# An encoder trunk on one core: ScalarE takes half of each look from turn 23 on, the two halves of the weight sums run one after the other, and outputs and mixes are reordered

## The chip, the cores and the metric

The kernel runs on one core of one Trainium2 chip. The metric is the device time of one execution in microseconds (us), taken as the median of several runs. A profiled execution gives a trace of every instruction of the five engines: PE (TensorE; PEld is its loading of weights), DVE (VectorE), ACT (ScalarE), POOL (GpSimd) and SP (SyncE, which issues the DMAs).

## The reference

For each of two sequences (prompt, 1024 tokens; sample, 2048 tokens) one layer is computed:

```python
h = rms_norm(x, norm_pre)
z = einsum('btd,de->bte', h, w_in)
u_pool, g_pool, q, k, v, g_attn, q_x, g_x = split(z)
pool_out = multiscale_pool(u_pool, pool_w, pool_scale) * silu(g_pool)
q, k = rope(rms_norm(q)), rope(rms_norm(k))        # 8 query heads, 2 key heads, 64 wide
attn_out = softmax(q k^T / 8) v * silu(g_attn)      # every query sees every key
x_out = softmax(q_x k_m^T / 8) v_m * silu(g_x)      # 256 memory tokens, 4 heads
y = einsum('bte,ed->btd', concat(pool_out, attn_out, x_out), w_out)
return x + rms_norm(y, norm_post)
```

## The kernel before

The first part (to 709 us) makes normed and transposed tokens, projects them with w_in and writes queries, keys, values and gates to scratch in HBM; the scheduler of the language orders it. The second part (attention, output projection) has its order written out by hand, one queue for each engine, and the change lies there.

A *pair* is 256 queries: the sample has 8 pairs, which go first, the prompt 4. A pair has three *groups*: kind 0 and kind 1 are the two halves of the self-attention heads, kind 2 is the memory attention; they run in the order 0, 2, 1 (2, 0, 1 in the first pair). A *turn* is two chunks of 128 keys of one group, so a sample pair has 8 + 1 + 8 = 17 turns and a prompt pair 4 + 1 + 4 = 9. Turn n issues, in this order on every engine:

- *look*: the softmax needs the largest score of each query before its weights are made. PE writes the scores of 128 queries with 512 keys for two heads into the tile N (1024 columns, two PSUM banks, one buffer), and DVE reduces them to the largest ones in `nb` (L191; `top` for kind 2). Two looks are made in a turn, for a group that comes later; the second is issued after the weights.
- `sums(kb+1)`: the odd chunk of the turn before is added to the running sum z of the weights. In the sample POOL adds the first 512 columns and DVE the other 512 (CUT = (0, 512), L235 and L236); in the prompt DVE adds all 1024.
- `weights(k)`, `weights(k+1)`: PE makes scores in the tile S, ACT makes P = exp(S) (L223; five buffers of P).
- the second look, then `sums(k)`.
- on one turn in two from turn 23 on a piece of the output projection into `py` (`project`, 4 pieces of 3 matmuls in the sample, 8 in the prompt; after its last piece ACT squares the bank, L386), on the other `values`: PE adds P times V of four chunks into `acc` (L248). Before turn 23 values of two chunks are made in every turn.
- one turn after a group's last, `totals`: PE multiplies the finished z by ones (L257). Columns 0 to 511 come first, and those are POOL's.

Work that hangs on a turn is put in by `at(turn + fraction, ...)`: fraction 0 before the first look, .1 after it, .4 before the projection, .6 at the turn's end. `take` multiplies `acc` by the gate (L263), `turned`, `inverse` and `spread` turn the totals into factors (L267, L272 and L275, then two DMAs by way of HBM, `rows` and `gz`), `mix_out` multiplies them in (L292, POOL) and `high` and `low` split the product for the projection (L295 ACT, L299 POOL). `scale`, `norm` and `out` finish an output tile (L398 DVE, L402 DVE and L405 POOL, L414 ACT and L415 POOL).

Of the kernel before, what the change touches and what calls it, by code (L numbers as in the profile page):

```python
# [23 lines left out]
def encoder(ctx, tc, I, O):  # L24
# [25 lines left out]
    DVM = [scratch(f"dvm{s}", [128, 2, 4, 64]) for s in range(2)]  # L50

    const = ctx.enter_context(tc.tile_pool(name="const", bufs=1))
    ident = const.tile([128, 128], F32, name="ident")
    make_identity(nc, ident)
    mhalf = const.tile([128, 8], F32, name="mhalf")
    nc.vector.memset(mhalf, -0.5)

    def rsqrt(pool, ss, n, count, tag):

# [71 lines left out]
    class Group:  # L131
# [36 lines left out]

        def largest(self, n):
            a, lane = self.pieces[n]
            S = psn.tile([128, 1024], F32, name="N", tag="N")
            if self.kind == 2:
                for x in range(2):
                    for j in range(2):
                        h = slice(64 * j, 64 * j + 64)
                        nc.tensor.matmul(S[:, 512 * j + 256 * x:512 * j + 256 * x + 256],
                                         lhsT=self.q[h, 0, 256 * lane + 128 * x:256 * lane + 128 * x + 128],
                                         rhs=K2[0][h, lane, 0], start=True, stop=True)  # L180
                S = S.rearrange("p (j x k) -> p j x k", j=2, x=2)
                out = self.top[:, 0:8].rearrange("p (j i x) -> p j i x", j=2, i=2)[:, :, lane]
            else:
                for j in range(2):
                    h = slice(64 * j, 64 * j + 64)
                    nc.tensor.matmul(S[:, 512 * j:512 * j + 512],  # L186
                                     lhsT=self.q[h, 0, 128 * lane:128 * lane + 128],
                                     rhs=KH[self.kind][h, 512 * a:512 * a + 512], start=True, stop=True)
                S = S.rearrange("p (j k) -> p j k", j=2)
                out = self.nb[:, a].rearrange("p (j i) -> p j i", j=2)[:, :, lane]  # L190
            nc.vector.tensor_reduce(out=out, in_=S, axis=AX.X, op=ALU.max, negate=True)  # L191
            if n == len(self.pieces) - 1:
                self.shift()

# [30 lines left out]
        def sums(self, k):  # L225
            if k == 0:
                return
            if k == 1:
                self.z = dbl.tile([128, 2, 512], F32, name="z", tag="z")
            flat = "p j q -> p (j q)"  # L230
            z, P = self.z.rearrange(flat), self.P[k].rearrange(flat)
            a = self.P[0].rearrange(flat) if k == 1 else z
            cut = CUT[self.s]
            if cut:
                nc.gpsimd.tensor_tensor(out=z[:, :cut], in0=a[:, :cut], in1=P[:, :cut], op=ALU.add)  # L235
            nc.vector.tensor_tensor(out=z[:, cut:], in0=a[:, cut:], in1=P[:, cut:], op=ALU.add)  # L236

        def values(self, ks):

# [48 lines left out]
    def store_mix(slot, pair, c, a, b, v="p (c t q) -> p c t q"):  # L288
# [11 lines left out]

        after = (0, 0, pair.s, pair.s)[c // 2]
        begin = max(slot, pair.free + after)
        at(begin + 1.4, high)
        at(begin + 1.6, low)

    class Pair:

# [39 lines left out]
    class Output:  # L347
# [34 lines left out]
            nc.tensor.matmul(ps, lhsT=ml, rhs=wo_hi[:, c, cols], start=False, stop=final)  # L382

        def square(self, h):
            junk = own.tile([128, 512], mybir.dt.bfloat16, name="junk2", tag="junk2")
            nc.scalar.activation(out=junk, in_=self.ps[h], func=AF.Square, scale=D ** -0.5,  # L386
                                 accum_out=self.ss[:, h:h + 1])

# [10 lines left out]

        def norm(self):  # L400
            s1 = dbl.tile([128, 1], F32, name="s1", tag="s1")
            nc.vector.scalar_tensor_tensor(out=s1, in0=self.ss[:, 0:1], scalar=EPS, in1=self.ss[:, 1:2],  # L402
                                           op0=ALU.add, op1=ALU.add)
            self.r = dbl.tile([128, 1], F32, name="rs", tag="rsy")
            nc.gpsimd.tensor_tensor(out=self.r, in0=s1, in1=mhalf[:, 0:1], op=ALU.pow)  # L405

# [54 lines left out]
    for pair in pairs:  # L461
# [5 lines left out]
        for g in pair.groups:  # L467
            wait = first[g] + g.chunks // 2 + (2 if pair.last else 3)
            if pair is pairs[0] and g.kind != 1:
                wait += 3  # L470
            at(wait + 0.6, g.mix_out, wait + 1, pair)
        at(max(ends) + (3 if pair.last else 7), open_fill, pair)
    value_runs, sums_at = {}, {}
    for g in groups:
# [4 lines left out]
        while k < c:  # L479
            run = 1 if 2 < n + k < first[pairs[1].groups[0]] + 6 else 2  # L480
            value_runs[n + k + run - 1] = g, list(range(2 * k, min(2 * k + 2 * run, 2 * c)))
            k += run
        at(n + max(c, run) + 0.1, g.take)
        sums_at[n + c] = g
        at(n + c + 1.1, g.turned)
        if g in pairs[-1].groups:
            at(n + c + (1.4 if g.kind < 2 else 2.1), g.inverse)
            at(n + c + (1.4 if g.kind < 2 else 2.1), g.spread)
        else:
            at(n + c + (1.4 if g.kind < 2 else 2.6), g.inverse)  # L490
            at(n + c + (2.1 if g.kind < 2 else 3.1), g.spread)
    for c in range(NC):
        at(int(2.5 * c + 1), load_w_out, c)
        for h in range(2):
# [32 lines left out]
    def look(turn):  # L527
        if looks.get(turn):
            g, n = looks[turn].pop(0)
            g.largest(n)  # L530

    order = {mybir.EngineType.PE, mybir.EngineType.Activation, mybir.EngineType.DVE,
             mybir.EngineType.Pool, mybir.EngineType.SP}
# [7 lines left out]

    with ExitStack() as p1:
        one = p1.enter_context(tc.tile_pool(name="p1one", bufs=1))
        two = p1.enter_context(tc.tile_pool(name="p1two", bufs=2))
        big = p1.enter_context(tc.tile_pool(name="p1big", bufs=2))

# [411 lines left out]
    def project(turn):  # L958
# [3 lines left out]
        for _ in range(PIECES[turns[turn][0].s] if turn < len(turns) else 8):  # L962
            out, h, c, start, final = fill.pop(0)
            out.piece(h, c, start, final, turn >= looked)
            if final:
# [4 lines left out]
                else:  # L970
                    at(turn + 1.1, out.scale, h)
                if h == 1:
                    at(turn + (0.6 if end else 1.6), out.norm)
                    for x in range(2):
                        if out.last:
                            at(turn + 0.6, out.out, x, None)
                        else:
                            at(turn + 2.4 + x, out.out, x, None if end else turn + 3.2 + x)
                break

    with tc.manual_schedule(engines=order):
# [69 lines left out]
```

## Time and profile before

| what | us |
|---|---|
| median of three runs | 1746.3 (1745.69 to 1746.43) |
| the profiled execution, device time | 1745.43 |
| its span from first to last instruction | 1743.6 |
| PE busy | 1697.3 (97%) |
| DVE busy | 1116.8 (64%) |
| POOL busy | 844.3 (48%) |
| ACT busy | 656.7 (38%) |

Busy PE does not mean PE at its peak: matmuls overlap, and one that starts late is drawn longer. So what PE loses is read from the distance between the starts of its matmuls, beside the list of waits. In the lists, "PEld N L186 <- DVE nb L191: 37.5, 88, 0.8" says that the weight loads of line 186 sat behind idle time 88 times, 37.5 us in all and 0.8 us at most, that a DVE instruction of line 191 ended.

### The profile page before, as it was taken

Reading aid. Unit: us, or ns where it says so; the run is one execution under the profiler, and the core shown is the slowest. Engines: PE = TensorE matmul, PEld = TensorE weight load, DVE = VectorE, ACT = ScalarE, POOL = GpSimd, SP = SyncE. Lnnn points to the kernel's source line nnn. Section 1 sums busy time; section 2 is a strip of 40 time slices with the busy share of each in tenths; the row PEclk is TensorE's granted clock in tenths of the full one; section 3 lists DMA queues with packets and bytes.
Section 4 is the critical chain, followed back from the end, with each engine's and each line's share of the span. In section 5 each row is a group of like instructions: output and inputs, shape, how many; then the busy total and the mean of one; then the engine's idle time right before and its main releaser. Section 6 shows DMA issues by size and latency. Waiting matters only on the chain. (4 is left out here: it accounts for less than half of the span.)

```text
span 1743.6 us, 25303 instructions
## 1 busy us (share of the span) xinstructions
PE 1697.3 (97%) x9400; PEld 1168.0 (67%) x9400; DVE 1116.8 (64%) x1434; ACT 656.7 (38%) x978; POOL 844.3 (48%) x778
## 2 busy tenths in 40 slices
PE   7899999999999999999999999999999999999998
PEld 6889889798898986544555555555555555566566
DVE  6754316552164424799878787877777757876862
ACT  5533225332252211445444344444343433443441
POOL 4555205570054610499666575767666663331331
PEclk9999999999999999999999999999999999999999
DMA  7643634436443393612121212112111143323222
GB/s 256 177 132 87 186 94 135 128 89 172 113 124 91 110 217 85 181 62 86 49 73 61 68 53 76 56 49 77 48 58 55 61 127 110 103 80 109 68 91 91
DMA packets 151851, 178.27 MB, mean 102 GB/s; under 512 B 20896, under 2 KB 120368, under 8 KB 151728
## 3 DMA queue, kind: packets, MB, share of 16 engines
q1 hardware_dynamic: 151728, 176.65, 34.0%
q8 instruction: 74, 1.21, 0.3%
q14 instruction: 49, 0.40, 0.1%
HBM read 121.26 MB, written 55.20 MB: 101 GB/s over the span
## 5 line engine op out<-in xcount | busy, mean ns | idle before, releaser
L191 DVE TENSOR_REDUCE nb<-N 128x2 f32<-128x1024 f32 x320 | 390.3, 1220 | 215.7 <-PE N L186 215.0
L223 ACT ACTIVATE P<-S 128x1024 f32<-128x1024 f32 x344 | 334.6, 1023 | 436.5 <-PE S L221 174.0
L235 POOL TENSOR_TENSOR z<-z,P 128x512 f32<-128x512 f32 x224 | 324.2, 1447 | 160.2 <-ACT P L223 140.4
L248 PE MATMUL acc<-P,V 128*64 128x512 f32 (+1 forms) x1472 | 320.3, 575 | 1.5
L236 DVE TENSOR_TENSOR z<-z,P 128x512 f32<-128x512 f32 (+1 forms) x272 | 269.3, 990 | 4.5 <-ACT P L223 4.3
L614 PE MATMUL pz<-hT_hi,w_hi 128*128 128x512 f32 x592 | 235.2, 397 | 1.7 <-ACT vmst L884 0.8
L615 PE MATMUL pz<-hT_lo,w_hi 128*128 128x512 f32 x592 | 232.8, 393 | 0.0
L616 PE MATMUL pz<-hT_hi,w_lo 128*128 128x512 f32 x592 | 231.5, 391 | 0.1
L248 PEld LDWEIGHTS acc<-P,V 128*64 128x64 f32 x1472 | 95.3, 137 | 170.7 <-issue 130.7
L221 PE MATMUL S<-q,DH 64*128 64x512 f32 x1280 | 201.6, 392 | 0.0
L63 POOL TENSOR_TENSOR rs<-rs,mhalf 128x4 f32<-128x4 f32 (+2 forms) x76 | 83.6, 1103 | 210.4 <-DVE rs L61 207.3
L186 PE MATMUL N<-KH,q 64*128 64x512 f32 x640 | 157.0, 487 | 12.4 <-DVE nb L191 11.0
L186 PEld LDWEIGHTS N<-KH,q 64*128 64x128 f32 x640 | 59.8, 183 | 153.2 <-DVE nb L191 86.4
L614 PE MATMUL pz<-w_hi,hT_hi 128*128 128x384 f32 (+1 forms) x416 | 141.6, 341 | 3.8 <-ACT hT_hi L68 3.8
L615 PE MATMUL pz<-w_lo,hT_hi 128*128 128x384 f32 (+1 forms) x416 | 140.7, 338 | 0.9 <-DVE w_lo L69 0.8
L616 PE MATMUL pz<-w_hi,hT_lo 128*128 128x384 f32 (+1 forms) x416 | 140.6, 339 | 0.0
L380 PE MATMUL py<-wo_hi,mix 128*128 128x512 f32 x336 | 139.0, 414 | 0.0
L69 DVE TENSOR_TENSOR w_lo<-wraw,w_hi 128x3072 fp32r<-128x3072 f32 (+2 forms) x21 | 67.8, 3227 | 107.3 <-ACT w_hi L68 106.9
L221 PEld LDWEIGHTS S<-q,DH 64*128 64x128 f32 x1280 | 120.1, 185 | 23.6 <-issue 2.4
L382 PE MATMUL py<-wo_hi,mix 128*128 128x512 f32 x336 | 131.6, 392 | 0.1
L381 PE MATMUL py<-wo_lo,mix 128*128 128x512 f32 x336 | 131.5, 391 | 0.0
L614 PEld LDWEIGHTS pz<-hT_hi,w_hi 128*128 128x128 f32 x592 | 111.1, 188 | 29.1 <-issue 4.5
(152 smaller groups left out, 2436.3 us busy)
## 6 DMA issues: line engine op xcount, KB each, us to landing
wraw<-w_in SPq DMA_DIRECT2D x15, 1536.0 KB
dg<-gst SPq DMA_DIRECT2D x48, 256.0 KB
q<-dq SPq DMA_DIRECT2D x24, 512.0 KB
gz<-rows SPq DMA_DIRECT2D x72, 128.0 KB
x<-x_sample SPq DMA_DIRECT2D x16, 512.0 KB
xr<-x_sample SPq DMA_DIRECT2D x16, 512.0 KB
y_sample<-xr SPq DMA_DIRECT2D x32, 256.0 KB
dq<-qst SPq DMA_DIRECT2D x96, 64.0 KB
```

The costliest lines, as they stand in the source:

```text
L186: nc.tensor.matmul(S[:, 512 * j:512 * j + 512], lhsT=self.q[h, 0, 128 * lane:128 * lane + 128], rhs=KH[self.kind][h, 512 * a:512 * a + 512 ...
L191: nc.vector.tensor_reduce(out=out, in_=S, axis=AX.X, op=ALU.max, negate=True)
L221: nc.tensor.matmul(S[:, at + x:at + x + w], lhsT=K, rhs=self.q[h, qx, x:x + w], start=False, stop=n == 2, skip_group_check=True)
L223: nc.scalar.activation(out=self.P[k].rearrange("p j q -> p (j q)"), in_=S, func=AF.Exp)
L235: nc.gpsimd.tensor_tensor(out=z[:, :cut], in0=a[:, :cut], in1=P[:, :cut], op=ALU.add)
L236: nc.vector.tensor_tensor(out=z[:, cut:], in0=a[:, cut:], in1=P[:, cut:], op=ALU.add)
L248: nc.tensor.matmul(self.acc[64 * j:64 * j + 64, x], lhsT=v, rhs=P[:, j, x], start=(k, i) == (0, 0), stop=k == self.chunks - 1, skip_group_ ...
L380: nc.tensor.matmul(ps, lhsT=mh, rhs=wo_hi[:, c, cols], start=first, stop=False)
L382: nc.tensor.matmul(ps, lhsT=ml, rhs=wo_hi[:, c, cols], start=False, stop=final)
L614: nc.tensor.matmul(ps, lhsT=sh, rhs=mh, start=c == 0, stop=False)
L615: nc.tensor.matmul(ps, lhsT=sh, rhs=ml, start=False, stop=False)
L616: nc.tensor.matmul(ps, lhsT=sl, rhs=mh, start=False, stop=c == n - 1)
```

## The change

Seven things are changed.

- From turn 23 on, a look of kind 0 or 1 is shared: ACT copies the second bank of N to a tile `look` in SBUF, DVE reduces the first bank from PSUM (half A) and then the copy (half B). `square` writes its unused output to the same tile.
- In `sums` DVE's half is issued first, and POOL's half waits for it (`behind`), in every chunk but a group's last.
- `norm` adds its two sums on POOL in place of DVE.
- In the prompt, `norm`, `out` and `store` come up to one turn sooner, and `high` and `low` of four of the eight columns about one turn sooner.
- `turned` of kinds 0 and 1 comes before the first look in place of after it; `take` of kind 2 at the end of its turn.
- `inverse` and `spread` of kind 2 come about one turn later, but for the last pair, and its `mix_out` one turn later.
- The identity for the transposes is kept in the first part's pool only.

```diff
+    def behind(later, first):
+        tc.add_manual_dep(later.ins, first.ins.name,
+                          mybir.DependencyInfo(mybir.DependencyClass.Sync, mybir.DependencyReason.DATA),
+                          reason="one after the other")
...
-        def largest(self, n):
+        def largest(self, n, shared=False):
...
-            nc.vector.tensor_reduce(out=out, in_=S, axis=AX.X, op=ALU.max, negate=True)
+            if shared and self.kind < 2:
+                t = own.tile([128, 1, 512], F32, name="look", tag="look")
+                c = nc.scalar.copy(out=t[:, 0], in_=S[:, 1])
+                m = nc.vector.tensor_reduce(out=out[:, 0:1], in_=S[:, 0:1], axis=AX.X, op=ALU.max, negate=True)
+                tc.declare_no_dep(m.ins, c.ins, reason="two reads, in two banks")
+                nc.vector.tensor_reduce(out=out[:, 1:2], in_=t, axis=AX.X, op=ALU.max, negate=True)
+            else:
+                nc.vector.tensor_reduce(out=out, in_=S, axis=AX.X, op=ALU.max, negate=True)
...
+            v = nc.vector.tensor_tensor(out=z[:, cut:], in0=a[:, cut:], in1=P[:, cut:], op=ALU.add)
             if cut:
-                nc.gpsimd.tensor_tensor(out=z[:, :cut], in0=a[:, :cut], in1=P[:, :cut], op=ALU.add)
-            nc.vector.tensor_tensor(out=z[:, cut:], in0=a[:, cut:], in1=P[:, cut:], op=ALU.add)
+                e = nc.gpsimd.tensor_tensor(out=z[:, :cut], in0=a[:, :cut], in1=P[:, :cut], op=ALU.add)
+                if k < self.chunks - 1:
+                    behind(e, v)
...
-        at(begin + 1.4, high)
-        at(begin + 1.6, low)
+        soon = pair.s == 0 and not pair.last and c < 4
+        at(begin + (0.6 if soon else 1.4), high)
+        at(begin + (0.6 if soon else 1.6), low)
...
-            junk = own.tile([128, 512], mybir.dt.bfloat16, name="junk2", tag="junk2")
+            junk = own.tile([128, 1, 512], F32, name="look", tag="look")[:, 0]
...
-            nc.vector.scalar_tensor_tensor(out=s1, in0=self.ss[:, 0:1], scalar=EPS, in1=self.ss[:, 1:2],
-                                           op0=ALU.add, op1=ALU.add)
+            nc.gpsimd.tensor_scalar(out=s1, in0=self.ss[:, 0:1], scalar1=EPS, scalar2=self.ss[:, 1:2],
+                                    op0=ALU.add, op1=ALU.add)
...
             if pair is pairs[0] and g.kind != 1:
                 wait += 3
+            elif g.kind == 2 and not pair.last:
+                wait += 1
...
-        at(n + max(c, run) + 0.1, g.take)
+        at(n + max(c, run) + (-0.4 if g.kind == 2 else 0.1), g.take)
         sums_at[n + c] = g
-        at(n + c + 1.1, g.turned)
+        at(n + c + (1.1 if g.kind == 2 else 1), g.turned)
...
-            at(n + c + (1.4 if g.kind < 2 else 2.6), g.inverse)
-            at(n + c + (2.1 if g.kind < 2 else 3.1), g.spread)
+            at(n + c + (1.4 if g.kind < 2 else 3.4), g.inverse)
+            at(n + c + (2.1 if g.kind < 2 else 4.1), g.spread)
...
-            g.largest(n)
+            g.largest(n, turn >= 23)
...
-                    at(turn + (0.6 if end else 1.6), out.norm)
+                    slow = not end and turns[turn][0].s == 1
+                    at(turn + (0.6 if end else 1.6 if slow else 1.4), out.norm)
...
-                            at(turn + 2.4 + x, out.out, x, None if end else turn + 3.2 + x)
+                            z = turn + (2.4 + x if slow else 1.6)
+                            at(z, out.out, x, None if end else z + 0.8)
```

The order on PE is the same in both kernels. DVE's queue in the fourth sample pair, from the first look of the turn that starts at 1002 us in the trace of before to the first look of kind 2 in the next turn (`nb<-N` is a look, `z<-z,P` a sum, `y<-py` a `scale`; the numbers tell buffers apart). Before:

```order
L191 TENSOR_REDUCE nb_8406<-N_8811 128x2 [waits PE_49]
L398 TENSOR_TENSOR y_8643<-py_8714,npost_6289 128x512 [waits Activation_49]
L236 TENSOR_TENSOR z_8645<-z_8645,P_8780 128x512 [waits DVE_49]
L191 TENSOR_REDUCE nb_8406<-N_8839 128x2 [waits PE_49]
L236 TENSOR_TENSOR z_8645<-z_8645,P_8823 128x512 [waits DVE_49,Activation_49]
L402 SCALAR_TENSOR_TENSOR s1_8859<-ssy_8527 128x1
L191 TENSOR_REDUCE top0_5597<-N_8863 128x2x2 [waits PE_49]
```

The same place after:

```order
L197 TENSOR_REDUCE nb_8535<-N_8997 128x1 [waits PE_49]
L199 TENSOR_REDUCE nb_8535<-look_9000 128x1 [waits Activation_49]
L411 TENSOR_TENSOR y_8808<-py_8888,npost_6289 128x512
L244 TENSOR_TENSOR z_8810<-z_8810,P_8963 128x512 [waits DVE_49]
L197 TENSOR_REDUCE nb_8535<-N_9028 128x1 [waits PE_49]
L199 TENSOR_REDUCE nb_8535<-look_9031 128x1 [waits Activation_49]
L244 TENSOR_TENSOR z_8810<-z_8810,P_9012 128x512 [waits DVE_49]
L201 TENSOR_REDUCE top0_5597<-N_9055 128x2x2 [waits PE_49]
```

Each look is two instructions now, of which the second waits for ACT, and the sum of norm's squares has left this queue.

POOL's queue of the same pair, from `norm` in the next turn to the last sum of kind 0 two turns later (the five sums are of chunks 11 to 15; `xr` is an `out`). Before:

```order
L405 TENSOR_TENSOR rs_8861<-s1_8859,mhalf_128 128x1 [waits DVE_49]
L235 TENSOR_TENSOR z_8645<-z_8645,P_8831 128x512 [waits Pool_49]
L235 TENSOR_TENSOR z_8645<-z_8645,P_8871 128x512 [waits Activation_49,Pool_49]
L415 TENSOR_TENSOR xr_8641<-xr_8641,y_8643 128x512 [waits DMAHW1_49,DMAHW6_49,DMAHW0_49,Activation_49]
L299 TENSOR_TENSOR mix_8846<-gate_8154,mix_8845 128x512
L299 TENSOR_TENSOR mix_8846<-gate_8228,mix_8845 128x512
L292 TENSOR_TENSOR pu_8819<-pu_8819,pg_8818 128x512 [waits DMAHW7_49,DMAHW1_49,DMAHW0_49]
L235 TENSOR_TENSOR z_8645<-z_8645,P_8879 128x512 [waits Pool_49]
L235 TENSOR_TENSOR z_8645<-z_8645,P_8929 128x512 [waits Activation_49,Pool_49]
L415 TENSOR_TENSOR xr_8641<-xr_8641,y_8643 128x512 [waits Activation_49]
L235 TENSOR_TENSOR z_8645<-z_8645,P_8937 128x512 [waits Pool_49]
```

The same place after:

```order
L415 TENSOR_SCALAR s1_9051<-ssy_8677 128x1
L418 TENSOR_TENSOR rs_9053<-s1_9051,mhalf_123 128x1 [waits Pool_49]
L246 TENSOR_TENSOR z_8810<-z_8810,P_9020 128x512 [waits DVE_49]
L246 TENSOR_TENSOR z_8810<-z_8810,P_9063 128x512 [waits DVE_49,Pool_49]
L428 TENSOR_TENSOR xr_8806<-xr_8806,y_8808 128x512 [waits DMAHW1_49,DMAHW6_49,DMAHW0_49,Activation_49]
L311 TENSOR_TENSOR mix_9038<-gate_8259,mix_9037 128x512
L311 TENSOR_TENSOR mix_9038<-gate_8339,mix_9037 128x512
L304 TENSOR_TENSOR pu_9008<-pu_9008,pg_9007 128x512 [waits DMAHW7_49,DMAHW1_49,DMAHW0_49]
L246 TENSOR_TENSOR z_8810<-z_8810,P_9071 128x512 [waits DVE_49,Pool_49]
L246 TENSOR_TENSOR z_8810<-z_8810,P_9124 128x512 [waits DVE_49,Activation_49,Pool_49]
L428 TENSOR_TENSOR xr_8806<-xr_8806,y_8808 128x512 [waits Activation_49]
L246 TENSOR_TENSOR z_8810<-z_8810,P_9132 128x512 [waits Pool_49]
```

The order is the same but for the added sum of norm. The sums of chunks 11 to 14 now wait for DVE's half of the same chunk; that of chunk 15 does not.

More of the change, by code (lines that the diff above doesn't have):

```diff
@@ L52, in encoder @@
     const = ctx.enter_context(tc.tile_pool(name="const", bufs=1))
-    ident = const.tile([128, 128], F32, name="ident")
-    make_identity(nc, ident)
     mhalf = const.tile([128, 8], F32, name="mhalf")
     nc.vector.memset(mhalf, -0.5)
+    def behind(later, first):
+        tc.add_manual_dep(later.ins, first.ins.name,
+                          mybir.DependencyInfo(mybir.DependencyClass.Sync, mybir.DependencyReason.DATA),
+                          reason="one after the other")
     def rsqrt(pool, ss, n, count, tag):
@@ L543, in encoder @@
         one = p1.enter_context(tc.tile_pool(name="p1one", bufs=1))
+        ident = one.tile([128, 128], F32, name="ident")
+        make_identity(nc, ident)
         two = p1.enter_context(tc.tile_pool(name="p1two", bufs=2))
```

## The prediction

> **What bounds the kernel now.** I read the page's busy shares first, then the busy time by stage, then what PE's weight loads waited for in each stage, and last the timeline of single turns. The page's first section and four stages (each row: stretch, its length, then PE, PEld, DVE, ACT and POOL busy, clock, DMA):
>
> ```profile
> PE 1697.3 (97%) x9400; PEld 1168.0 (67%) x9400; DVE 1116.8 (64%) x1434; ACT 656.7 (38%) x978; POOL 844.3 (48%) x778
> ...
> 709.00:822.00 113.00, 106.32 (x644) 49.16 (x645) 102.98 (x108) 58.12 (x70) 95.68 (x64) 1.00 0.40 119
> 822.00:1395.00 573.00, 571.28 (x3382) 320.19 (x3382) 451.63 (x529) 240.71 (x299) 373.73 (x270) 1.00 0.18 60
> 1395.00:1470.00 75.00, 72.08 (x427) 39.93 (x426) 48.51 (x61) 29.72 (x36) 40.65 (x30) 0.98 0.44 131
> 1470.00:1662.00 192.00, 186.37 (x1122) 114.21 (x1122) 150.06 (x171) 74.28 (x103) 54.21 (x41) 1.00 0.27 87
> ```
>
> PE is the bound and its order does not change, so a gain can come only from PE's waits and from matmuls that start late. The stages are the turns up to 23, the sample pairs with shared looks, the step from sample to prompt, and the prompt pairs. Waits of PE's weight loads from 822 to 1395, and below them one from 1470 to 1662:
>
> ```profile
> PEld N L186 <- DVE nb L191: 37.5, 88, 0.8
> PEld acc L257 <- POOL z L235: 3.0, 5, 0.6
> ...
> PEld N L186 <- DVE nb L191: 14.5, 24, 1.3
> ```
>
> Nearly every turn has a look that waits for the one before it: N has one buffer. One such turn on PE, DVE and ACT (start, length, engine and line):
>
> ```profile
> 1002.02 0.50 PE L186 MATMUL N<-KH,q 64*128 64x512 f32 x2
> 1002.56 1.23 DVE L191 TENSOR_REDUCE nb<-N 128x2 f32<-128x1024 f32 x1 [1.45 <-PE N L186]
> 1003.30 1.94 ACT L223 ACTIVATE P<-S 128x1024 f32<-128x1024 f32 x2 [0.49 <-issue]
> 1003.51 0.39 PE L221 MATMUL S<-q,DL 64*128 64x512 f32 x2
> 1003.84 0.49 PE L186 MATMUL N<-KH,q 64*128 64x512 f32 x2
> 1004.26 3.65 PE L248 MATMUL acc<-P,V 128*64 128x512 f32 x16
> 1004.30 0.68 DVE L236 TENSOR_TENSOR z<-z,P 128x512 f32<-128x512 f32 x1
> 1004.90 1.22 DVE L191 TENSOR_REDUCE nb<-N 128x2 f32<-128x1024 f32 x1
> 1006.03 0.68 DVE L236 TENSOR_TENSOR z<-z,P 128x512 f32<-128x512 f32 x1
> ```
>
> The first look's reduction ends at 1003.79 and the second look starts 0.05 us later; from the last weights matmul to `acc` it is 4.26 - 3.51 = 0.75 us. A turn in which the reduction was done 0.43 us early:
>
> ```profile
> 1121.53 1.23 DVE L191 TENSOR_REDUCE nb<-N 128x2 f32<-128x1024 f32 x1 [2.44 <-PE N L186]
> ...
> 1122.95 0.40 PE L221 MATMUL S<-q,DL 64*128 64x512 f32 x2
> 1123.19 0.39 PE L186 MATMUL N<-KH,q 64*128 64x512 f32 x2
> 1123.51 0.87 PE L248 MATMUL acc<-P,V 128*64 128x256 f32 x6
> ```
>
> There it is 3.51 - 2.95 = 0.56 us. A blocked second look costs 0.19 us.
>
> **The change part by part.** Prices first, each as least, median and longest (ns): a copy of a bank by ACT, a reduction of 256 or 384 columns from SBUF, the two halves of a sum, and norm's sum on DVE.
>
> ```profile
> L783 ACT COPY u<-pz x12: 567/585/632, 100.6 to 553.8; 128x512 f32<-128x512 f32 x12
> L678 DVE TENSOR_REDUCE ssh<-sq x48: 405/478/555, 52.4 to 610.5; 128x4 f32<-128x256 f32 x24, 128x6 f32<-128x384 f32 x24
> L235 POOL TENSOR_TENSOR z<-z,P x224: 1262/1297/1817, 720.5 to 1453.5; 128x512 f32<-128x512 f32 x112
> L236 DVE TENSOR_TENSOR z<-z,P x272: 649/727/2232, 723.3 to 1700.6; 128x512 f32<-128x512 f32 x112, 128x1024 f32<-128x1024 f32 x24
> L402 DVE SCALAR_TENSOR_TENSOR s<-ssy x24: 116/151/1228, 865.9 to 1738.2; 128x1 f32<-128x1 f32 x24
> ```
>
> *Shared looks.* Each adds a copy (0.59 us, ACT, which is 42% busy from 822 to 1395) and turns 1.22 us of DVE into two halves. A half is not in the trace: from below half of 1.22, 0.61, from above the sum over 512 columns, 0.68 to 0.73. I take 0.68, so DVE gains 0.15 us of work in each look. Half A ends at 1002.56 + 0.68 = 1003.24 and the copy, with ACT idle until 1003.30, near 1003.2: the second look is free some 0.5 us before PE reaches it at 1003.74. The first look of the next turn has room too: the second copy follows the two exponentials, 1005.24 + 0.59 = 1005.83, and the next turn starts after 1007.8. In the sample 88 waits at 0.19 us are 16.7 us; I take 15 for looks at which DVE is late by more than the 0.5 us. Ends: 0 and 17.
>
> What a copy in SBUF does beside GpSimd, the traces of before do not tell, since the reductions of L678 run in another stage. If GpSimd stopped half B as it stops sums, DVE would wait up to 1.26 us in some looks. The Trainium skill ("SBUF — State Buffer", Who interferes with whom) says that on trn2 a reduction never contends with GpSimd, and a two-input sum in SBUF does. By that rule half B stays at its price, and the gain of this step stays 15 us; without it some 5 us of it could go.
>
> *Sums in order.* DVE's half comes first and POOL's waits for it. Where POOL has time this costs nothing: its 1.26 us lies beside the next look, and the two no longer collide. Where POOL has none, it is late. POOL in the fourth sample pair from chunk 10's sum to chunk 15's, and the totals on PE that read it:
>
> ```profile
> 1004.47 1.64 POOL L235 TENSOR_TENSOR z<-z,P 128x512 f32<-128x512 f32 x1 [2.21 <-PE N L186]
> 1006.07 1.77 POOL L299 TENSOR_TENSOR mix<-pu,mix 128x512 fp32r<-128x512 f32 x1
> ...
> 1009.05 0.55 POOL L405 TENSOR_TENSOR rs<-s,mhalf 128x1 f32<-128x1 f32 x1
> ...
> 1023.35 1.28 POOL L235 TENSOR_TENSOR z<-z,P 128x512 f32<-128x512 f32 x1
> ...
> 1024.68 0.64 PE L257 MATMUL acc<-z,ones 128*32 128x256 f32 x8 [0.19 <-POOL z L235]
> ```
>
> From 1004.47 to 1024.63 POOL has no gap, and PE is waiting for its last sum already. Now chunk 10's sum waits for DVE's, which ended at 6.71 before. After, it is behind half B of the second look: 1005.83 + 0.05 + 0.68 + 0.68 = 1007.2. POOL's sum ends near 1008.5 in place of 1006.1, 2.4 us late, and nothing behind it has slack: the same queue to 1024.63 is 18.5 us, norm's sum adds 0.4 (between the 0.15 that DVE took and the 0.55 of the `rs` beside it), and I take off 0.7 for two collisions fewer (1.64 and 1.77 against 1.26). It ends at 1008.5 + 18.5 + 0.4 - 0.7 = 1026.7. PE, with three second looks at 0.19 saved, gets there at 1024.49 - 0.57 = 1023.9: a wait of 2.8 us where there was 0.2. I take 2.3 more, since a late POOL meets DVE's sums at other places; ends 0 and 3.5. It comes once in each of the third to eighth sample pairs (five waits to 1395, one after): 6 x 2.3 = 14 us lost, ends 0 and 21.
>
> *Turns up to 23.* PE's weight loads waited there so:
>
> ```profile
> PEld N L186 <- DVE nb L191: 25.6, 35, 1.6
> PEld acc L248 <- ACT P L223: 19.7, 38, 0.7
> ```
>
> Looks stay whole, DVE is 91% busy and POOL 85%, for POOL also splits w_out. Two sums and a part of w_out at 1.26 us on POOL and two sums at 0.65 on DVE, which stop each other, are at most 3 x 1.26 + 2 x 0.65 = 5.1 us, and the 113 us hold 24 turns of 4.7. Ordered, POOL cannot work ahead: of those 0.4 us I take 0.3, in some seven turns with both, 2 us lost. Ends: 3 us gained, if DVE's sums no longer collide, and 6 lost, if it is so in 20 turns.
>
> *Kind 2's `inverse` later, `take` and `turned` sooner.* At the end of the sample DVE's transpose into `gz` waits for a POOL product that waits for a DMA, with the looks queued behind it:
>
> ```profile
> 1424.61 0.45 DVE L275 STREAM_TRANSPOSE gz<-rz 128x256 f32<-128x256 f32 x1 [4.14 <-POOL gate L292]
> ...
> 1426.22 0.66 PE L186 MATMUL N<-KH,q 64*128 64x512 f32 x2 [2.24 <-DVE nb L191]
> ```
>
> A turn later the product is done. That is 2.2 us of PE, and the values that follow, short of P by then, and the blocked looks nearby give the rest: 4 us gained, ends 1 and 5. The DMAs `rows` and `gz` move a turn down SP's queue past a load of `q` three turns ahead of its use: nothing.
>
> *Prompt.* DVE makes all of a sum, so ordering changes nothing there. Norm's sum leaves DVE, where POOL's mixes stopped it:
>
> ```profile
> 1553.25 1.08 DVE L402 SCALAR_TENSOR_TENSOR s<-ssy 128x1 f32<-128x1 f32 x1
> 1554.26 1.21 DVE L191 TENSOR_REDUCE nb<-N 128x2 f32<-128x1024 f32 x1
> ...
> 1555.52 0.50 PE L186 MATMUL N<-KH,q 64*128 64x512 f32 x2 [0.89 <-DVE nb L191]
> ```
>
> 24 waits at 0.19 are 4.6 us. They last 14.5/24 = 0.60 us on average where those of the sample last 37.5/88 = 0.43, and that excess, 24 x 0.17 = 4.1 us, is lost whole: 8.7 us. Against it DVE, 78% busy, gets 0.3 us more a turn and waits for the second copy. I take 7 us gained, ends 9 gained and 4 lost. Outputs and mixes sooner are work off PE, hidden by POOL, 28% busy here.
>
> *The rest.* Norm's sum on POOL stands in the last chain: 0.3 us lost. The identity moves no time.
>
> Sum: -15 + 14 + 2 - 4 - 7 + 0.3 = -9.7 us. From the profiled execution's 1745.4 (span 1743.6 and 1.8 around it) that is 1735.7; the median of the runs is 0.9 above that execution, so 1736.6.
>
> **The rivals.** (A) POOL's lateness is hidden: its sums, now 1.26 us and not up to 1.82, catch up before the totals. For it: the excess over 1.26 us in those rows; against it: no gap in 20 us. Then 1736.6 - 14 = 1722.6.
>
> (B) Slower: the ordered sums hold POOL so long that totals wait 5 us in each of six pairs, for each sum of the pair's last four waits anew for a DVE that POOL itself has stopped. It decides from 2.3 + 9.7/6 = 3.9 us per pair on. For it: DVE's sums, 0.65 us at least, lasted up to 2.2; against it: while PE waits, both catch up. 1736.6 + 6 x 2.7 = 1753.
>
> (C) The shared look does not free N: ACT comes to its copy late, behind a square or an output scale that waits for POOL, and PE waits as before. Against it: ACT is 42% busy there. Without the 15 us, 1751.6.
>
> (D) No change: PE is 97% busy, and the waits moved equal those removed: 1746, if totals wait 3.9 us.
>
> (E) DVE becomes the bound in the prompt by its 0.15 us a look; the 7 us are not gained: 1743.6. The Trainium skill ("Perfetto Trace Analysis", Optimizing Scalar/DVE Operations) has both rules: larger operations where an engine is saturated, smaller ones where an unsaturated engine causes bubbles. At 78% the trace leaves open which holds here.
>
> **How the numbers follow.** Mine 0.45, A 0.20, B 0.13, C 0.05, D 0.07, E 0.10. About 0.2% (3.5 us) is what a measurement can tell: faster means under 1742.8. Mine (but for 0.01), A and half of E make 0.69 faster; D, the rest of E and 0.01 make 0.13 same; B and C 0.18 slower. My case's own range, with 1.5 to 3 us at the totals and 3 to 9 in the prompt, is 1728 to 1743; the whole takes in A to 1720 and C to 1752.
>
> **What would show it.** Right: second looks 0.56 us before the next group's start and few waits for `nb` from 822 on; totals of kind 0 waiting 2 to 3 us for POOL in six pairs; no wait of several us at `gz`. Wrong: totals with under 1 us (A) or over 4 (B); `N` waiting for ACT (C); second looks in the prompt that still wait for DVE (E).

## The result and the profile after

The changed kernel takes 1758.11 us (median of 7 runs, 1752.18 to 1761.92) where the kernel before took 1745.69 us in the same runs (7 runs, 1743.25 to 1750.28). The ratio is 1.0067, with a 95% interval of 1.0045 to 1.0088: slower by 0.7%, where 0.6% faster was forecast. The profiled execution took 1756.4 us, and its span is 1754.5 us against 1743.6 before.

The page's busy times, and the four stages (boundaries put where PE is at the same instruction as in the rows shown of before):

```profile
PE 1686.4 (96%) x9400; PEld 1173.4 (67%) x9400; DVE 1122.1 (64%) x1668; ACT 792.3 (45%) x1236; POOL 830.9 (47%) x802
```

```profile
709.00:829.00 120.00, 107.15 (x644) 49.80 (x640) 104.00 (x108) 57.50 (x69) 90.65 (x64) 0.99 0.39 113
829.00:1408.00 579.00, 563.30 (x3379) 323.73 (x3380) 452.06 (x706) 341.38 (x490) 352.66 (x277) 0.98 0.18 59
1408.00:1483.00 75.00, 71.14 (x430) 40.47 (x430) 50.81 (x78) 38.66 (x53) 43.87 (x35) 0.98 0.47 135
1483.00:1674.00 191.00, 183.39 (x1122) 114.60 (x1122) 149.85 (x213) 99.39 (x152) 63.66 (x49) 1.00 0.28 89
```

Two stages grew: the turns up to 23 (113 to 120 us) and the sample pairs (573 to 579 us). In the second one PE is busy for 8 us less than before, and its granted clock, the figure behind POOL's, is 0.98 where it was 1.00. The waits of PE's weight loads, first from 709 to 829 us, then from 829 to 1408 us:

```profile
PEld N L189 <- DVE nb L201: 27.3, 37, 1.6
PEld acc L260 <- ACT P L233: 18.6, 37, 0.7
PEld py L269 <- POOL z L246: 5.6, 2, 3.1
PEld py L395 <- POOL mix L311: 3.8, 2, 3.3
...
PEld acc L269 <- POOL z L246: 17.8, 5, 3.6
...
PEld acc L260 <- ACT P L233: 12.0, 42, 0.3
```

The 88 waits of a look for `nb` (37.5 us) are gone from the second list. In their place PE's totals wait for POOL's sums, 3.6 us each by the weight loads. One turn, and then POOL and PE around the totals of the fourth sample pair:

```profile
1008.62 0.59 ACT L196 COPY look<-N 128x512 f32<-128x512 f32 x1
...
1009.24 0.69 DVE L199 TENSOR_REDUCE nb<-look 128x1 f32<-128x512 f32 x1 [0.22 <-ACT look L196]
1009.29 0.39 PE L231 MATMUL S<-q,DL 64*128 64x512 f32 x2
1009.51 0.39 PE L189 MATMUL N<-KH,q 64*128 64x512 f32 x2
1009.83 3.65 PE L260 MATMUL acc<-P,V 128*64 128x512 f32 x16
...
1013.30 1.28 POOL L246 TENSOR_TENSOR z<-z,P 128x512 f32<-128x512 f32 x1 [0.72 <-DVE z L244]
...
1017.64 0.86 POOL L415 TENSOR_SCALAR s<-ssy 128x1 f32<-128x1 f32 x1
...
1030.64 1.26 POOL L428 TENSOR_TENSOR xr<-xr,y 128x512 f32<-128x512 f32 x1
1031.86 1.26 POOL L246 TENSOR_TENSOR z<-z,P 128x512 f32<-128x512 f32 x1
...
1033.17 1.08 PE L269 MATMUL acc<-z,ones 128*32 128x256 f32 x8 [3.13 <-POOL z L246]
...
1036.06 0.63 PE L231 MATMUL S<-q,DL 64*128 64x512 f32 x2
```

From the last weights matmul (at 1009.29) to `acc` it is 9.83 - 9.29 = 0.54 us: the second look between them is not blocked any more. POOL has no gap of more than 0.1 us from chunk 10's sum at 1013.30 to chunk 15's, which ends at 1033.12, and PE stands 3.13 us. And behind the wait a pair of `S` matmuls is drawn 0.63 us long where it was 0.39. The same stretch in windows of 2 us (the first figure behind POOL's is the clock):

```profile
1032.00:1034.00 2.00, 0.83 (x8) 0.20 (x8) 0.00 (x0) 0.00 (x0) 2.00 (x2) 0.67 0.33 131
1034.00:1036.00 2.00, 2.00 (x12) 1.48 (x10) 1.42 (x3) 0.59 (x1) 0.35 (x1) 0.50 0.43 119
1036.00:1038.00 2.00, 2.00 (x12) 1.54 (x10) 1.60 (x3) 1.02 (x1) 0.00 (x0) 0.50 0.71 274
1038.00:1040.00 2.00, 2.00 (x12) 0.91 (x12) 0.69 (x1) 1.50 (x2) 0.00 (x0) 0.63 0.00 0
```

By these rows 3.4 us of full clock are missing, so PE runs at half its clock for some 6.8 us. In the clock's records of the trace it is so for 3.41 us behind five of the six waits at the totals, and for 6.83 us behind this one; in the trace of before the clock is 1.00 at those places.

Since PE's order is the same, the two traces can be laid over each other start by start. After minus before, in us:

| stretch | predicted | measured |
|---|---|---|
| first part, to the first matmul of the second | 0 | -0.8 |
| turns up to 23, to the projection that starts at 826 us | +2 | +7.7 |
| looks and moved steps of the sample, waits at the totals and half clock taken out | -15 | -16.8 |
| six waits at the totals of kind 0 (3.13 to 3.62 us each, 0.14 to 0.56 before) | +14 | +17.9 |
| half clock behind them (sized by e2_filled) | none | +10.0 |
| step from sample to prompt, without its wait at the totals | -4 | -5.0 |
| prompt | -7 | -1.1 |
| tail behind the last matmul | +0.3 | -1.0 |
| sum (spans 1754.5 and 1743.6) | -9.7 | +10.9 |

### The profile page after: what moved, and what is told of

Read it like the earlier page. It is cut to its first block, busy times and chain, and to the rows that moved or that the text cites. A ratio compares the mean times of both kernels' runs of the same rounds, so it can differ in the third digit from the quotient of the medians.

```text
span 1754.5 us, 26096 instructions
## 1 busy us (share of the span) xinstructions
PE 1686.4 (96%) x9400; PEld 1173.4 (67%) x9400; DVE 1122.1 (64%) x1668; ACT 792.3 (45%) x1236; POOL 830.9 (47%) x802
## 3 DMA queue, kind: packets, MB, share of 16 engines
q8 instruction: 75, 1.23, 0.3%
## 5 line engine op out<-in xcount | busy, mean ns | idle before, releaser
L233 ACT ACTIVATE P<-S 128x1024 f32<-128x1024 f32 x344 | 335.2, 1024 | 122.3 <-PE S L231 106.8
L246 POOL TENSOR_TENSOR z<-z,P 128x512 f32<-128x512 f32 x224 | 299.3, 1336 | 161.0 <-DVE z L244 145.2
L196 ACT COPY look<-N 128x512 f32<-128x512 f32 x258 | 152.0, 589 | 202.6 <-PE N L189 202.0
L197 DVE TENSOR_REDUCE nb<-N 128x1 f32<-128x512 f32 x258 | 176.6, 684 | 74.1 <-PE N L189 73.8
L231 PE MATMUL S<-q,DH 64*128 64x512 f32 x1280 | 205.5, 399 | 0.0
L199 DVE TENSOR_REDUCE nb<-look 128x1 f32<-128x512 f32 x258 | 175.7, 681 | 43.2 <-ACT look L196 42.3
L189 PE MATMUL N<-KH,q 64*128 64x512 f32 x640 | 148.9, 461 | 8.5 <-DVE nb L201 4.3
```

The source lines that it names most:

```text
L189: nc.tensor.matmul(S[:, 512 * j:512 * j + 512], lhsT=self.q[h, 0, 128 * lane:128 * lane + 128], rhs=KH[self.kind][h, 512 * a:512 * a + 512 ...
L197: m = nc.vector.tensor_reduce(out=out[:, 0:1], in_=S[:, 0:1], axis=AX.X, op=ALU.max, negate=True)
L199: nc.vector.tensor_reduce(out=out[:, 1:2], in_=t, axis=AX.X, op=ALU.max, negate=True)
L231: nc.tensor.matmul(S[:, at + x:at + x + w], lhsT=K, rhs=self.q[h, qx, x:x + w], start=False, stop=n == 2, skip_group_check=True)
L233: nc.scalar.activation(out=self.P[k].rearrange("p j q -> p (j q)"), in_=S, func=AF.Exp)
L246: e = nc.gpsimd.tensor_tensor(out=z[:, :cut], in0=a[:, :cut], in1=P[:, :cut], op=ALU.add)
```

## The experiments

All medians, in us; the ratio is to the kernel before in the same runs.

| run | median (lowest to highest) | ratio, 95% interval |
|---|---|---|
| e1_free | 1728.9 (1727.5 to 1729.8) | 0.9902 (0.9888 to 0.9916) |
| e2_filled | 1752.2 (1750.1 to 1754.4) | 1.0037 (1.0023 to 1.0051) |
| e3_late_only | 1749.2 (1744.5 to 1754.1) | 1.0015 (1.0001 to 1.0028) |
| e4_order_only | 1775.0 (1773.0 to 1777.7) | 1.0169 (1.0152 to 1.0185) |
| e5_looks_only | 1737.8 (1736.7 to 1738.7) | 0.9956 (0.9944 to 0.9969) |
| e6_sample_looks | 1729.1 (1727.9 to 1731.3) | 0.9908 (0.9894 to 0.9922) |
| e7_prompt_unmoved | 1728.1 (1726.2 to 1728.6) | 0.9899 (0.9885 to 0.9912) |
| e8_out_after | 1721.3 (1720.5 to 1723.5) | 0.9860 (0.9845 to 0.9876) |
| e9_norm_on_dve | 1736.5 (1734.1 to 1738.2) | 0.9944 (0.9932 to 0.9956) |
| e10_order_early_chunks | 1739.5 (1734.9 to 1740.3) | 0.9958 (0.9945 to 0.9970) |
| e11_inverse_early | 1728.7 (1727.8 to 1730.9) | 0.9902 (0.9889 to 0.9915) |
| e12_take_turned_late | 1729.6 (1728.7 to 1730.5) | 0.9906 (0.9893 to 0.9918) |
| e13_changed_out_after | 1750.3 (1747.1 to 1753.0) | 1.0024 (1.0015 to 1.0033) |
| e14_order_7_chunks | 1725.0 (1721.1 to 1727.2) | 0.9871 (0.9854 to 0.9889) |

**e1_free: the change without the ordering.**

```diff
-                if k < self.chunks - 1:
-                    behind(e, v)
```

> Changed kernel without the wait of POOL's sums for DVE's; everything else as changed. Theory M (the ordered sums cost the time, and the shared looks do save it): compared start by start, the ordered sums took 7.7 us up to 826 us, 6 x 3.0 us of waits at the totals and 6 x 1.6 us of half clock behind them, so 1758.1 - 7.7 - 18 - 9.7 = 1723 us (1720 to 1730); the totals of kind 0 wait under 0.7 us for POOL, and the clock is 1.00 from 822 to 1395. Rival R (the copy on ScalarE and the two half reductions make POOL and DVE late): within 4 us of 1758, with the totals still waiting about 3 us.

1728.9 us: the ordering alone cost 29.2 us and hid a gain of 18 us. Laid over each other, the trace after is behind that of e1_free by 8.2 us at 826 us, by 6 x 2.0 us more in the waits at the totals and by 9.8 us elsewhere up to 1400 us (most of it half clock), and by nothing more from there on. Behind none of e1_free's waits does the clock fall. Not as expected: the totals still wait 1.16 us in five pairs (7.9 us by the weight loads, below), since PE now comes earlier.

```profile
PEld acc L267 <- POOL z L246: 7.9, 5, 1.6
```

**e2_filled: PE kept at work during the wait.** The wait stays; only the standing still is taken out of it.

```diff
+            if self.kind == 0 and self.s == 1 and not self.early and self.p > 1:
+                for _ in range(12):
+                    nc.tensor.matmul(self.zt, lhsT=wo_hi[:, 0, 0:128], rhs=wo_hi[:, 0, 0:512],
+                                     start=True, stop=True)
```

> Changed kernel with 12 matmuls of w_out by itself (2.8 us, result unused) put on PE ahead of the totals of kind 0 in the third to eighth sample pairs, where PE otherwise stands 3.1 us for POOL. Theory C (standing still is what brings the granted clock down to 0.50 for some 4 us): no drop behind the totals any more, 6 x 1.6 us gained, 1748.5 us (1746 to 1751). Rival (the drop is set by something else at that place, such as the transfers or the load of the engines): drops stay, and the time is 1758 or a little more.

The fourth pair's totals again, and the clock behind them:

```profile
1031.14 2.88 PE L270 MATMUL acc<-wo_hi 128*128 128x512 f32 x12
1034.51 0.64 PE L272 MATMUL acc<-z,ones 128*32 128x256 f32 x8 [0.49 <-POOL z L246]
```

```profile
1034.50:1038.50 4.00, 3.99 (x36) 2.59 (x38) 3.27 (x6) 2.47 (x4) 1.19 (x1) 1.00 0.58 193
```

No drop is left at the six places, and between the two traces PE gains there 1.4, 2.8, 1.4, 1.5, 1.4 and 1.5 us, 10.0 in all. It is the standing still that lowers the clock. The medians differ by 5.9 us only, so the time lies 1.2 us beyond the range that was expected. In the profiled execution 2.5 us were lost again behind the wait of 2.9 us at 826 us, and 1.4 us at the start of the prompt behind one of 1.74 us; neither brought a drop in the trace after.

The records of the clock show why. In each of the sixteen traces every stretch of half clock begins on one grid of 3.41 us, and the grid lies otherwise in each execution. Windows of this grid around the wait at 826 us, in the changed kernel:

```profile
821.03:824.45 3.42, 2.18 (x16) 1.15 (x12) 3.42 (x3) 2.94 (x4) 3.34 (x3) 1.00 0.00 0
824.45:827.86 3.41, 1.72 (x7) 1.11 (x7) 2.11 (x3) 0.03 (x1) 3.41 (x4) 1.00 0.08 19
827.86:831.27 3.41, 3.41 (x22) 2.23 (x24) 1.82 (x3) 1.64 (x3) 3.33 (x3) 1.00 0.19 59
```

And in e2_filled:

```profile
822.29:825.70 3.41, 1.11 (x8) 0.55 (x6) 3.38 (x4) 2.40 (x4) 3.33 (x3) 1.00 0.00 0
825.70:829.11 3.41, 2.82 (x7) 2.24 (x8) 1.09 (x1) 0.00 (x0) 3.41 (x3) 0.50 0.27 77
```

In the first execution the grid splits the wait, and PE stands for 1.24 and 1.69 us of two windows (length less PE's busy time). In the second 2.30 us of it fall into one window, and the next one has half clock. So the same wait at the same place is followed by half clock in one execution and not in another; the last section counts all windows.

**e3_late_only: no ordering in the first four groups.**

```diff
-                if k < self.chunks - 1:
+                if k < self.chunks - 1 and self.n > 3:
```

> Changed kernel with POOL's sums waiting for DVE's only from the second sample pair's memory attention on (the first four groups unordered). Theory M (in the early turns too it is the ordering that made POOL late): the waits of 1.6, 2.2 and 2.9 us for POOL at 757, 796 and 826 us go, 1758.1 - 7.7 = 1750.4 us (1748 to 1753), and the later waits of 3 us stay. Rival (POOL is late there because turned, take and the shared look of turn 23 on come in other order): within 3 us of 1758.

1749.2 us, 8.9 less; before 822 us the waits of `py` for POOL's `z` are 1.6 us in all, as in the kernel before, and 5.6 in the changed one. The early loss is the ordering's.

**e4_order_only: the ordering alone, on the kernel before.**

```diff
+            v = nc.vector.tensor_tensor(out=z[:, cut:], ...)
             if cut:
-                nc.gpsimd.tensor_tensor(out=z[:, :cut], ...)
-            nc.vector.tensor_tensor(out=z[:, cut:], ...)
+                e = nc.gpsimd.tensor_tensor(out=z[:, :cut], ...)
+                if k < self.chunks - 1:
+                    behind(e, v)
```

> Kernel before with DVE's half of the sum first and POOL's waiting for it, and nothing else. Theory M: early turns 7.7 us lost; from 850 us on POOL's chunk 10 ends 1.9 us late in place of 2.4, since the looks stay whole, and PE comes to the totals as late as before, so they wait 1.3 to 1.8 us and the clock holds: 1745.7 + 7.7 + 6 x 1.4 = 1762 us (1757 to 1768). Rival R (the shared looks make POOL late): at most 1750 us.

1775.0 us: 28 us lost, more than the 16 expected, and as much as with the shared looks (29.2). By the starts, 8.8 us go up to 826 us and 1.5 us in each pair at the totals, as reckoned. What was not reckoned with are the looks: one look in each pair waits 1.5 to 1.6 us for `nb`, and from 850 to 1395 us late second looks take some 25 us where they took some 16. The waits from 822 to 1395 us:

```profile
PEld N L191 <- DVE nb L196: 36.6, 74, 2.0
...
PEld acc L264 <- POOL z L241: 10.2, 5, 2.1
```

Which of VectorE's instructions come late there was not taken apart.

**e5_looks_only: the shared looks alone, on the kernel before** (the edit of `largest` and of `look(turn)` in the diff above, the tile for it, and with it the move of the identity).

> Kernel before with the shared looks from turn 23 on (and the tile they need), and no other part of the change. Theory M (the looks are worth what their waits were): blocked second looks go from 850 to 1395 us, 16 us gained, less 5 x 0.5 us that PE, now earlier, waits longer at the totals; the wait of 2.2 us at 1426 us stays; the prompt gives 5 us back and loses up to 5: 1747.0 - 13.5 = 1733.5 us (1729 to 1738). Rival (what e1_free gained came mostly from the moved steps): 1740 us or more.

1737.8 us, 8 us gained where 13.5 were expected. The missing part stands in the look of kind 2 (fourth pair):

```profile
1005.67 1.74 POOL L304 TENSOR_TENSOR mix<-gate,mix 128x512 fp32r<-128x512 f32 x1
...
1006.18 1.24 DVE L407 SCALAR_TENSOR_TENSOR s<-ssy 128x1 f32<-128x1 f32 x1
...
1007.34 1.21 DVE L196 TENSOR_REDUCE top<-N 128x4 f32<-128x1024 f32 x1
...
1008.61 0.51 PE L176 MATMUL N<-K,q 64*128 64x256 f32 x4 [1.01 <-DVE top L196]
```

Norm's sum of two numbers takes 1.24 us beside POOL's mix, the look is queued behind it, and PE waits 1.01 us for it in five pairs and 0.89 in one. Before, DVE had the look early enough for that.

**e6_sample_looks: whole looks in the prompt** (e1_free with `23 <= turn < first[pairs[8].groups[0]]` for `turn >= 23`).

> e1_free with the looks shared only in turns of the sample; the prompt's are whole again. Theory E (the two halves make DVE late in the prompt): the waits for top (1.03 us) and for the second looks go, at 1725 us or less. Theory P (the prompt loses by its moved outputs, and the halves gain): blocked second looks come back, 24 x 0.19 us and more, and the other waits stay: 1732 to 1736 us.

**e7_prompt_unmoved: the prompt's outputs and mixes at their old places** (e1_free with `soon = False` and `slow = not end`).

> e1_free with the moves in the prompt undone (norm, out, store and the early high and low at their old places). Theory P (the two outs in a row hold POOL for 3.5 us, and DVE's 1024-wide sum beside them takes 1.94 us in place of 1.21, which makes the looks of kind 2 late): the waits of 1.03 us for top fall back to 0.24 and those of 0.5 to 0.8 at second looks go: 1728.9 - 4.5 = 1724.4 us (1722 to 1727). Theory E (the halves are to blame): within 1.5 us of 1728.9.

1729.1 and 1728.1 us against 1728.9. e7 lies where theory E put it, but e6, for which theory E forecast 1725 us or less, contradicts it, and theory P missed both. (With the second `out` of a tile and its store, the move in the prompt is 1.8 turns, not one.) From 1450 to 1650 us, e1_free, then e6, then e7:

```profile
PEld N L181 <- DVE top L201: 5.0, 4, 1.5
...
PEld N L181 <- ACT y L425: 2.4, 3, 0.8
```

```profile
PEld N L189 <- DVE nb L201: 12.3, 22, 1.0
...
PEld N L181 <- DVE top L201: 2.6, 4, 0.8
```

```profile
PEld N L189 <- ACT look L196: 3.7, 4, 1.5
...
PEld N L181 <- DVE top L201: 2.9, 4, 0.7
```

Each version takes away a wait and brings another: the waits of 1.03 us for `top` fall to 0.31 in both, but whole looks bring back 22 waits for `nb`, and the old places bring waits for ACT's copy. In the prompt neither the looks nor the moves are worth anything singly, and together 1.1 us by the table above; no run takes back both at once, and why the waits balance so closely stays open.

**e8_out_after: POOL's add of `out` behind the last sum** (on e1_free).

```diff
-                            z = turn + (2.4 + x if slow else 1.6)
+                            z = turn + ((2.4, 4.2)[x] if slow else 1.6)
```

> e1_free with the second out of an output tile in the sample, and its store, 0.8 of a turn later, so that POOL's add of 1.26 us stands behind the last sum of kind 0 and not ahead of it. Theory Q (the totals of kind 0 wait 1.16 us because POOL's queue is too long by that add): the waits fall to about 0, 5 x 1.1 + 1.2 = 6.7 us gained: 1722.2 us (1720.5 to 1725). Rival (the last sum waits for something else, such as the weights or DVE): within 1.5 us of 1728.9.

1721.3 us. The totals wait 0.06 us in five pairs and 0.52 in the sixth, where it was 1.16 and 1.61. POOL's queue ahead of that sum is what sets the wait, one to one. This version beats the changed kernel by 36.9 us and the one before by 1.4%.

**e9_norm_on_dve: norm's sum back on VectorE** (on e8_out_after).

> e8_out_after with norm's sum of two numbers back on VectorE, as in the kernel before. Theory N (the shared looks need it off VectorE: POOL's mix stops it for 1.24 us there, with the look of kind 2 queued behind, and PE waits 1.01 us for top, as the trace of e5_looks_only shows in six pairs): 1721.3 + 6 x 1.05 = 1727.5 us (1726 to 1729.5). Rival (the wait for top came from the moved steps of e5_looks_only alone): within 1.5 us of 1721.3.

1736.5 us, 9 more than expected. Laid over e8_out_after, the waits of 1.01 us for `top` are back (0.89 in the third pair), 6.2 us in all, as theory N has it. The prompt loses 4 us more: there a look's copy stands behind ACT's `y`, which waits for norm, and PE waits 1.75 us twice, both times with half clock behind. The tail loses 1.3 us. And 1.7 us of the profiled difference of 14.4 lie in the first part, which is the same in both; some 1 us was not placed.

**e10_order_early_chunks: the ordering in chunks 1 to 9 only** (on e8_out_after).

```diff
+                if k < 10 and self.n > 3 and self.kind < 2:
+                    behind(e, v)
```

> e8_out_after with POOL's sums waiting for DVE's in chunks 1 to 9 only, in groups of kinds 0 and 1 from the second pair on; there POOL has gaps of 1.8 to 3.2 us in the trace. Theory M (ordering costs nothing where POOL has time, and gains nothing where PE does not wait for DVE): within 1.5 us of 1721.3, and no wait for POOL over 0.6 us at the totals. Rival (ordering costs at any place, since it lengthens the way from weights to sum): 1724 us or more.

1739.5 us: theory M fails, and the time is in the rival's range. The totals wait 1.83 to 1.91 us (2.30 in the sixth pair), and half clock follows four of the six times. POOL's queue in e8_out_after and here:

```profile
997.72 1.27 POOL L246 TENSOR_TENSOR z<-z,P 128x512 f32<-128x512 f32 x1 [2.34 <-ACT P L233]
999.55 1.28 POOL L309 TENSOR_TENSOR mix<-pu,mix 128x512 fp32r<-128x512 f32 x1 [0.56 <-ACT mix L305]
```

```profile
1002.59 2.97 POOL L246 TENSOR_TENSOR z<-z,P 128x512 f32<-128x512 f32 x2 [1.99 <-DVE z L244]
1005.52 1.28 POOL L311 TENSOR_TENSOR mix<-pu,mix 128x512 fp32r<-128x512 f32 x1
```

PE stands 3.85 us later here, so the first mix is 5.97 - 3.85 = 2.1 us late. Chunk 9's sum, the last one ordered, waits 2 us for DVE, chunk 10's queues behind it, and the mix, ahead of which POOL had a gap of 0.56 us, is pushed into the 20 us without one.

**e14_order_7_chunks: the same up to chunk 7** (`k < 8`).

> e10_order_early_chunks with the ordering only up to chunk 7. In its trace chunk 9's sum, the last ordered one, stood 2 us for VectorE and went straight into POOL's backlog. Theory L (only an ordered sum that borders on the backlog costs): the totals wait under 0.6 us for POOL, within 2 us of 1721.3. Rival (ordering costs wherever it stands): 1727 us or more.

1725.0 us, 1.7 more than theory L allows and 2 short of the rival. Its trace is on the side of L: the totals wait as in e8_out_after (3.3 us in all by the weight loads, against 3.4), and of the 3.3 us between the two traces 2.8 are there before the second part begins. By the traces, then, an ordered sum costs where nothing behind it can give, and some 0.5 us in all elsewhere; the medians leave room for up to 3.7.

**e11_inverse_early and e12_take_turned_late** undo two of the moves on e8_out_after: kind 2's `inverse`, `spread` and `mix_out` go back to 2.6, 3.1 and one turn earlier; `take` and `turned` go back to 0.1 and 1.1.

> e8_out_after with inverse, spread and mix_out of kind 2 at their old places. Theory T (they are moved out of the way of one wait, at the step from sample to prompt): the wait of 2.2 us for nb near 1410 us comes back, with up to 1.7 us of half clock behind it: 1721.3 + 2.3 to 4 = 1724.5 us (1723 to 1726). Rival (VectorE, with its shorter looks, is early enough there): within 1.5 us of 1721.3.

> e8_out_after with take of kind 2 and turned of kinds 0 and 1 at their old places (behind the first look). Compared start by start, PE's values came 0.47 us sooner behind take in six pairs and 0.30 us sooner behind turned in some eight places in e1_free than in e5_looks_only. Theory: 6 x 0.47 + 8 x 0.30 = 5.2 us lost: 1726.5 us (1724 to 1728). Rival (those steps are taken up by other waits): within 1.5 us of 1721.3.

1728.7 and 1729.6 us, both slower and by more than expected (7.5 and 8.4 us; the profiled executions lie 5.0 and 5.4 us apart, since that of e8_out_after was 2.2 us above its median). In the trace of the first the wait is back at 1411 us (2.14 us, and no half clock that time), which is 2.3 us. The second loses 0.46 us behind `take` in five sample pairs and 0.42 in one, and 0.30 to 0.34 us behind `turned` in twelve places; from 709 us to the end it falls 4.6 us behind; its waits from 822 to 1395 us are shown below. What else makes up the two differences was not found.

```profile
PEld acc L258 <- DVE rz L277: 6.1, 12, 0.7
...
PEld acc L258 <- DVE gate L273: 5.0, 6, 0.8
```

**e13_changed_out_after: the changed kernel, ordering and all, with e8's edit.**

> The changed kernel, ordering and all, with the second out of the sample and its store 0.8 of a turn later, so that POOL's add of 1.26 us no longer stands ahead of the last sum of kind 0. Theory L (POOL's lateness at the totals adds up one to one, and the half clock behind a wait grows rarer as the wait grows shorter): waits of 3.13 us fall to 2.0, 6 x 1.15 = 6.9 us, and of six stretches of half clock some two go, 3.4 us: 1758.1 - 10.3 = 1747.8 us (1743 to 1752). Rival (the ordering itself sets the wait, whatever stands in POOL's queue): within 2 us of 1758.

1750.3 us, 7.8 less. The waits at the totals are 2.03 us in place of 3.13 (2.51 in the sixth), and half clock follows four of the six. A shorter wait pays twice: by itself, and by the clock.

## Why the prediction was wrong

Forecast and trace lie 20.6 us apart. By the table, 10.0 us of it are half clock, 5.9 the prompt, 5.7 the turns up to 23 and 3.9 the waits at the totals; the other rows took 4.9 back. That it came out slower is what rival B forecast (1753 us), but not for B's reason.

- **Sums in order, +14: the mechanism was right and the size nearly.** The prediction had chunk 10's sum end 2.4 us late, nothing behind it with slack, and PE wait 2.8 us. The trace has 3.13 (3.62 in the sixth pair): 17.9 us in place of 14. One size in it was low: norm's sum on POOL, put at 0.4 us, lasted 0.81 to 0.86 us ahead of these six totals (0.86 in the rows above). Of rival B, a wait of 5 us as DVE and POOL stop each other, nothing is seen. Its sign, a sum of up to 2.2 us on DVE, was one over 1024 columns; over 512 columns the longest of before lasted 1.85 us.
- **Missing: the clock behind such a wait.** No term stood for it, and the row was there: behind the wait of 2.24 us at 1426 us the granted clock of that stage was 0.98, and I put it down to values short of P; in the clock's records 3.41 us of half clock follow that wait. e2_filled shows 10.0 us at the six places. So a pair pays (17.9 + 10.0)/6 = 4.65 us, which is beyond the 3.9 us from which the prediction said it would come out slower.
- **Turns up to 23, +2: wrong in size, since lateness was averaged over turns.** The prediction counted 0.3 us in some seven turns, as if a late sum were made good in the next turn. POOL was 85% busy there, and lateness runs on to the next reader: totals at 757 us (1.63 us) and 796 us (2.19 us, and half clock), the projection at 826 us (2.89 us). 7.7 us; e3_late_only gains 8.9.
- **Shared looks, -15: right in the whole change (-16.8, moved steps included), but not by itself.** From 850 to 1395 us 75 of 91 second looks started within 0.1 us of the end of a reduction, and none of 90 does after; what they lost falls from some 16 us to under 2. Half A and half B last 0.68 us, as taken:

```profile
L199 DVE TENSOR_REDUCE nb<-look x258: 659/685/687, 830.1 to 1677.0; 128x1 f32<-128x512 f32 x129
```

No half B is stretched beside POOL, as the Trainium skill ("SBUF — State Buffer", Who interferes with whom) has it of reductions; norm's sum (1.24 us in the rows of e5_looks_only, 0.12 at the least) and DVE's sums with two inputs (up to 1.80 us over 512 columns, 0.65 at the least) are. But e5_looks_only gains 8 us, since the look of kind 2 comes late there. Norm's sum on POOL (e9) and `take` and `turned` sooner (e12) are what keep the 15; I costed the one as a loss of 0.4 us on POOL and the others not at all.
- **Transition, -4: right.** The wait at `gz` is gone (5.0 us with the looks nearby; e11 brings 2.3 of it back).
- **Prompt, -7: wrong, -1.1.** Rival E had the sum right (nothing gained) and the cause in part: second looks there no longer wait for `nb`, but `top` waits 1.03 us where it waited 0.24, and others wait for ACT. e6 and e7 show that neither part alone moves the time; why stays open.
- **Tail, +0.3: wrong in sign.** Norm's sum on POOL no longer stands behind DVE's two `y`: it starts 0.1 us after the square's last step on ACT in place of 1.2, and the tail is 1.0 us shorter.

## What to carry to other kernels

An order imposed between two engines is paid where the second one's queue runs without a gap to its next reader; the lateness arrives there whole, however many turns later, so follow it to that reader and do not average it over turns. Price a wait of PE twice: its length, and behind it 1.4 to 2.8 us of half clock when more than about half of a window of 3.41 us goes by without a matmul. Since the grid of windows lies otherwise in each execution, that is a chance: 13 in 55 for waits of 1.2 to 1.95 us, and 12 in 13 beyond 3 us. A step that shortens one queue's waits may need small, quick instructions moved out of that queue before it gains: test such parts together and singly.

## What the runs showed of the hardware

The sixteen traces (before, after and the experiments) hold 176 stretches of 0.9 us and more between 709 and 1690 us in which PE had no matmul. Of 88 under 1.2 us none was followed by a lower clock within 8 us; of 55 from 1.2 to 1.95 us 13 were (one more stands just ahead of a gap of 2.46 us and is not counted), of 20 from 1.95 to 3.0 us 14, and of 13 beyond 3.0 us 12. The granted clock was then 0.50 for 3.41 us (33 times) or 6.83 us (six times), which cost 1.4 to 1.5 us or 2.5 to 2.8 us where it was measured.

The 39 drops follow from where the gaps fall on the grid of 3.41 us. Each execution, cut into windows of its own grid from 705 to 1700 us, gives 4605 windows that begin at full clock. The next window had half clock after all 30 in which PE had no matmul for more than 1.88 us, after 9 of the 15 with 1.71 to 1.88 us, and after none of the other 4560. The half clock lasted a second window the six times that PE stood for 0.51 us or more in the first one, and never at 0.46 us or less. So a gap of 3.13 us that the grid splits into 1.36 and 1.78 us, as once in e3_late_only, passes without a drop, and one of 1.23 us with other short gaps in its window (1.90 us in all, e6_sample_looks) does not. The Trainium skill ("TensorE: Matmul & The Clock Gate", Why this matters for your kernels) warns of gaps over some 3 us, and its section What's actually happening speaks of a free-running window of some 3.4 us. The grid of 3.41 us agrees with such a window; the threshold does not, since gaps of 1.7 us, and once one of 1.23 us, brought half clock here too, and about half a window was enough; the measurement decides.
